# Durations from the trace as the prices of an emitter's clocks

## The chip, the cores and the metric

The kernel runs on one core of one Trainium2 chip. The metric is the device time of one execution in microseconds (us), and of several executions the median.

## The reference

One step of a hybrid trunk of two layers. It serves 1024 sample positions and 128 prompt positions, here side by side as 1152 columns of width D = 1024, all in float32. Layer 0 joins latent attention (MLA) and a two-way retention behind one input projection; layer 1 is a chunked gMLP. A SwiGLU channel mixer of width 2816 follows in each.

```python
for l in range(DEPTH):
    ... = ada_mod(c, w_ada[l], b_ada[l])
    hs = modulate(rmsnorm(xs, norm_g[l, 0]), sh1s, sc1s)
    if l % 2 == 0:
        ys = ab_latent(hs, cache_mla_ckv[:, j], ..., w_in_ab[j], w_uq[j], w_ukv[j], ..., w_o_ab[j])
    else:
        ys = chunk_gmlp(hs, w_in_c[j], ln_g_c[j], ..., w_out_c[j])
    xs = xs + g1s * ys
    hs = modulate(rmsnorm(xs, norm_g[l, 1]), sh2s, sc2s)
    xs = xs + g2s * swiglu(hs, w_ffn_gate[l], w_ffn_up[l], w_ffn_down[l])
y_sample = rmsnorm(xs, final_norm_g)
```

The prompt columns go through the same steps with their own modulation. In the attention of layer 0 the normed latents are multiplied by `w_uq` (queries) and `w_ukv` (keys and values).

## The kernel before

Each float32 operand of a product is kept as a high part and a low part, and each product of a tile is three matmuls (high by high, high by low, low by high). The high part is a ScalarE cast, the low part a VectorE (or GpSimd) subtraction. Weights come from memory through three staging buffers (`ST`) and are split into a ring of five (`w0` to `w4`). The columns are worked in chunks of 384 or in pieces of 288. The channel mixer uses a scheme of seven products on half-size blocks, whose operands are sums that VectorE and GpSimd prepare.

The program is emitted by Python functions, and each engine does its instructions in the order in which they were emitted. That order isn't written out by hand. `Clocks` (L45) keeps a clock for each engine (T TensorE, V VectorE, S ScalarE, G GpSimd, Y the transfers' issue, D the transfers): `Clocks.op` (L76 to L114) gives every emitted instruction a start (its operands ready, its output free, its engine free) and a price. `Timed` (L117) sits between the emitter and the engines, so nearly every instruction of the profile has its line, L129. Nothing else of the program's timing is decided by these clocks but the place of background work:

- `fill` (L361), called between products, adds steps of three queues of generators as long as the VectorE and ScalarE clocks are no more than `ahead` past TensorE's: 7.0 us as a rule, 3.0 in the first part of the mixer, 1.5 at its end. It asks `bg3` (sums of squares), then `bg2` (the query products `upq`, L1270), then `bg` (all else).

```python
now = max(clk.t["T"], clk.ready(aps))
if not q or max(clk.t["V"], clk.t["S"], clk.t["G"] - 1.0) > now + ahead[0]:
    continue
```

- `Stream.pump` (L234) splits a weight when its clock says that the transfer has landed.
- The first stage (`advance` and the loop behind it, from L1169) picks among its tasks the one that can start first.
- `drain` (L356) and `bg_step` (L349) do not ask the clocks: they emit what is left of a generator at once, where its result is needed.

`upkv` (L1228) makes the keys and values of the attention: 26 groups of three matmuls, each evicted from PSUM into one of three buffers (`KVB`) and stored from there to `knd`, `kncd`, `vd` or `vpd`. It is background work of `bg`; behind the four gate units of the retention stands `drain(ck["kvdone"])`. At the very end `last1` and `done1` (L2469, L2475) take sums of squares of the final columns, and multiply by the reciprocal root; `done1` of the first half of the columns is background work too, of the second half it is drained.

Of the kernel before, what the change touches and what calls it, by code (L numbers as in the profile page):

```python
# [7 lines left out]
F32 = mybir.dt.float32  # L8
# [34 lines left out]
class Clocks:  # L43
# [33 lines left out]
    def op(self, e, name, args, kw):  # L77
        aps = [a for a in list(args) + list(kw.values()) if hasattr(a, "tensor")]
        out = kw.get("out", aps[0])
        ins = [a for a in aps if a is not out]  # L80
        t = max(self.t[e], self.ready(ins, e), self.free([out], e))
        n = 1
        for d in (ins[0] if name == "reduce_max" else out).shape[1:]:
            n *= d
        if "dma" in name:
            self.t[e] = t + (0.4 if e == "S" else 0.06)
            size = n * out.shape[0] * 4
            t = max(t + DMA_LAT, self.t["D"])
            self.t["D"] = t + size / 360e3
            end, e = self.t["D"] + DMA_LAT, "D"  # L90
        else:
            if e == "T":
                c = n / 2400 * (2 if name == "transpose" else 4 if ins[0].dtype == F32 else 1) + 0.014
                if out.shape[0] == 32:
                    c /= 4
                if t < PE_COLD:
                    c *= 2
            elif e == "V":
                psum = any(a.space == bass.MemoryType.PSUM for a in aps)
                c = (0.13 if psum else 0.065) + n / 960 * (6 if name == "reciprocal" else 1)  # L100
            elif e == "S":
                c = max(0.09 + n / 1200, 0.19)
                f = next((a for a in args if a in TABLES), None) if name == "activation" else None
                if f and f != self.table:
                    self.table = f
                    t += 1.28
            else:
                c = 0.16 + n / 480
            self.t[e] = t + c
            end = t + c  # L110
        for k in self.keys(out):
            self.w[k] = end, e
        for a in ins:
            for k in self.keys(a):  # L114
                self.r[k] = max(self.r.get(k, (0.0, e)), (end, e))
# [17 lines left out]
def body(nc, tc, ap):  # L133
# [473 lines left out]
    def rplaces(c):  # L607
        if c == 0:
            free = [hq_place(z, 0) for z in range(8)] + [flat_place(HF[z // 2], z % 2) for z in range(6)]
            for op in range(7):  # L610
                RIGHT[op, c] = free[2 * op:2 * op + 2]
        else:
            for n, op in enumerate((0, 1, 3, 5)):
                RIGHT[op, c] = [hq_place(2 * n + g, 1) for g in range(2)]
# [18 lines left out]
    def rsplit(c, todo):  # L633

        b11, b21, b12, b22 = ([xp2(2 * q + g, c, h) for g in range(2)] for h in range(2) for q in range(2))
        src = (b11, b21, b22, b11, b12, b22, b21)
        diff = dict(T1=(b11, b12, b11), T3=(b12, b22, b12), T2=(b22, b22, b11), T4=(b21, b21, b22))
        for z in todo:
            for g in range(2):
                if z in diff:  # L640
                    V.tensor_tensor(*(a[g] for a in diff[z]), ALU.subtract)
                    yield
                    continue
                op = int(z[1])
                if z[0] == "C":
                    if c and g == 0 and op in (2, 4, 6):
                        RIGHT[op, c] = x_places(op // 2 - 1)
                    S.copy(R(RIGHT[op, c][g][:, 0]), src[op][g])
                else:
                    hi, lo = (RIGHT[op, c][g][:, a] for a in range(2))  # L650
                    V.tensor_tensor(R(lo), src[op][g], hi, ALU.subtract)
                    if g:
                        normed.add((op, c))
                    yield
# [1893 lines left out]
```

## Time and profile before

| | us |
|---|---|
| median of 3 runs | 2855.09 |
| lowest and highest run | 2851.97, 2859.27 |
| the profiled execution | 2860.08 |
| its span in the trace | 2858.0 |
| TensorE busy | 2702.6 |
| VectorE busy | 1789.8 |
| ScalarE busy | 1168.2 |
| GpSimd busy | 514.3 |

The profiled execution is one run of its own, above the slowest of the three others by 0.81 us. In the rows below PE is TensorE's matmul, PEld its weight load, DVE VectorE, ACT ScalarE, POOL GpSimd and SP the engine that issues most transfers. A time in square brackets is how long the engine was idle before the row, and behind the arrow stands what ended that. Tiles stand without the numbers of their buffers (`hq`, `h`, `x`, `SC`, `w`).

### The profile page before, as it was taken

What the parts mean: (1) busy time and instruction counts of PE and PEld (TensorE: products, weight loads), DVE (VectorE), ACT (ScalarE), POOL (GpSimd) and SP (SyncE); (2) the same over time, 40 slices, a digit from 0 to 9 for tenths busy, and PEclk for the clock granted to TensorE, in tenths of its full rate; (3) what the DMA queues carried; (4) which work ended last, traced back from release to release, by engine and by line L of the source; (5) the groups of instructions that cost most, each with busy time, mean ns of one, the idle gap of its engine ahead of it and who ended that gap; (6) DMA issues with size and microseconds to landing.
All of it is one profiled execution on the core that took longest, in us unless ns stands there. A gap on an engine that the chain in (4) does not pass through costs nothing.

```text
span 2858.0 us, 49003 instructions
## 1 busy us (share of the span) xinstructions
PE 2702.6 (95%) x18859; PEld 2552.9 (89%) x18859; DVE 1789.8 (63%) x3606; ACT 1168.2 (41%) x2389; POOL 514.3 (18%) x570
## 2 busy tenths in 40 slices
PE   7999998999999999999999999998999999999996
PEld 5987897988999999999899877798899999999995
DVE  5661234888577566655788772455666666558876
ACT  5542223777455333433322351234544343332224
POOL 1120012665200000000465400000000000016550
PEclk8999998999999999999999999999999999999997
DMA  9386425323523444447878442352344343578761
GB/s 299 85 267 206 138 72 167 88 75 90 159 90 116 160 152 160 159 151 252 279 222 270 139 162 81 96 169 90 111 125 161 111 160 122 187 259 270 230 208 67
DMA packets 455328, 457.67 MB, mean 160 GB/s; under 512 B 25963, under 2 KB 399478, under 8 KB 453558
## 3 DMA queue, kind: packets, MB, share of 16 engines
q1 hardware_dynamic: 400272, 360.83, 41.1%
q10 hardware_dynamic: 54822, 93.70, 8.9%
q8 instruction: 149, 2.44, 0.4%
q14 instruction: 85, 0.70, 0.1%
HBM read 312.52 MB, written 141.93 MB: 159 GB/s over the span
## 4 chain that ended last, share of the span: by engine, by line
PE 70%; DVE 10%; DMA 5%; ACT 4%; issue 3%; POOL 1%; ACTq 0%; SPq 0%; DVEq 0%; POOLq 0%
PE PS L129 70%; DVE x L129 4%; DVE SC L129 2%; DVE w L129 2%; DMA hcd<-SC 2%; ACT x L129 1%; ACT w L129 1%; ACT SC L129 1%; DVE hq L129 1%; DMA ST<-in_w_ada 1%; POOL ST L129 1%; DMA w<-krd 0%; DMA rgd<-SC 0%; DMA w<-knd 0%; DMA ST<-in_w_in_c 0%
## 5 line engine op out<-in xcount | busy, mean ns | idle before, releaser
L129 PE MATMUL PS<-hq,w 128*128 128x288 f32 (+1 forms) x10644 | 1554.4, 303 | 57.9 <-ACT w L129 15.9
L129 PEld LDWEIGHTS PS<-hq,w 128*128 128x128 f32 x10644 | 1492.1, 190 | 93.0 <-ACT w L129 21.2
L129 DVE TENSOR_TENSOR w<-ST,w 128x512 fp32r<-128x512 f32 (+3 forms) x539 | 384.2, 730 | 292.6 <-ACT w L129 288.0
L129 ACT CAST w<-ST 128x512 fp32r<-128x512 f32 (+3 forms) x717 | 375.3, 552 | 424.1 <-POOL ST L129 277.0
L129 DVE SCALAR_TENSOR_TENSOR x<-PS,mod,x 128x288 f32<-128x288 f32 (+2 forms) x944 | 389.2, 445 | 125.1 <-PE PS L129 120.2
L129 POOL TENSOR_TENSOR w<-ST,w 128x256 fp32r<-128x256 f32 (+1 forms) x178 | 126.3, 726 | 1591.8 <-ACT w L129 970.1
L129 PE MATMUL PS<-h,w 128*128 128x288 f32 (+1 forms) x2522 | 389.2, 299 | 9.6 <-DVE SC L129 6.3
L129 PEld LDWEIGHTS PS<-h,w 128*128 128x128 f32 (+1 forms) x2522 | 353.1, 190 | 20.2 <-DVE SC L129 8.8
L129 ACT COPY SC<-PS 128x576 f32<-128x576 f32 (+8 forms) x245 | 124.3, 510 | 266.6 <-PE PS L129 219.3
L129 PE MATMUL PS<-x,w 128*128 128x288 f32 (+1 forms) x1440 | 219.9, 300 | 3.0 <-ACT adac L129 2.0
L129 PEld LDWEIGHTS PS<-x,w 128*128 128x128 f32 x1440 | 204.4, 189 | 4.9 <-ACT h L129 2.4
L129 DVE TENSOR_TENSOR SC<-PS,SC 128x576 f32<-128x576 f32 (+3 forms) x145 | 93.6, 647 | 167.3 <-PE PS L129 152.0
L129 POOL TENSOR_TENSOR ST<-ST 128x256 f32<-128x256 f32 (+1 forms) x192 | 140.4, 731 | 151.5 <-DVE w L129 134.7
L129 PEld LDWEIGHTS PS<-w,hq 128*128 128x128 f32 x648 | 120.4, 188 | 38.8 <-issue 11.4
L129 PE MATMUL PS<-w,hq 128*128 128x512 f32 x648 | 154.5, 396 | 0.0
L129 DVE TENSOR_TENSOR SC<-SC 128x288 f32<-128x288 f32 (+5 forms) x215 | 104.9, 496 | 63.4 <-ACT SC L129 47.4
L129 ACT ACTIVATE SC<-SC 128x576 f32<-128x576 f32 (+2 forms) x89 | 56.9, 639 | 194.0 <-DVE SC L129 182.1
L129 PE MATMUL PS<-w,w 96*128 96x512 f32 x384 | 109.6, 421 | 6.2 <-DMA w<-krd 2.7
L129 DVE TENSOR_TENSOR SC<-SC,x 128x576 fp32r<-128x576 f32 (+1 forms) x90 | 68.1, 757 | 68.4 <-DMA hcd<-SC 50.0
L129 DVE TENSOR_REDUCE sm<-PS 128x1 f32<-128x1152 f32 (+1 forms) x72 | 89.1, 1237 | 25.7 <-PE PS L129 25.0
L129 ACT ACTIVATE SC<-x 128x288 f32<-128x288 f32 x128 | 55.2, 440 | 118.1 <-DVE x L129 95.6
L129 DVE TENSOR_TENSOR ST<-ST 128x512 f32<-128x512 f32 x144 | 98.9, 687 | 1.8
(191 smaller groups left out, 2486.1 us busy)
## 6 DMA issues: line engine op xcount, KB each, us to landing
hq<-hcd SPq DMA_DIRECT2D x106, 576.0 KB, 8.9
hcd<-x ACTq DMA_DIRECT2D x180, 288.0 KB, 2.2
ST<-in_w_ada SPq DMA_DIRECT2D x80, 512.0 KB, 4.2
h<-hcd SPq DMA_DIRECT2D x48, 576.0 KB, 7.2
ST<-in_w_ffn_gate SPq DMA_DIRECT2D x52, 512.0 KB, 3.9
ST<-in_w_ffn_up SPq DMA_DIRECT2D x52, 512.0 KB, 4.0
hcd<-SC ACTq DMA_DIRECT2D x72, 288.0 KB, 3.3
ST<-in_w_ffn_down SPq DMA_DIRECT2D x80, 256.0 KB, 5.0
```

The source lines that it names most:

```text
L129: return fn(*args, **kw)
```

## The change

Only the prices in `Clocks.op` change. A matmul costs at least 0.11 us; one whose output has 32 rows is priced as one pass and not as a quarter of its price. A VectorE instruction has 0.16 us plus a 960th of its elements, and 0.05 more with three inputs, in place of 0.13 (an operand in PSUM) or 0.065. A ScalarE instruction has 0.2 us plus elements by 1250, in place of 0.09 plus elements by 1200 and at least 0.19. GpSimd has 0.22 plus elements by 460, in place of 0.16 and 480.

```diff
             if e == "T":
-                c = n / 2400 * (2 if name == "transpose" else 4 if ins[0].dtype == F32 else 1) + 0.014
+                c = max(n / 2400 * (2 if name == "transpose" else 4 if ins[0].dtype == F32 else 1) + 0.014, 0.11)
                 if out.shape[0] == 32:
-                    c /= 4
+                    c = n / 2400 + 0.014
                 if t < PE_COLD:
                     c *= 2
             elif e == "V":
-                psum = any(a.space == bass.MemoryType.PSUM for a in aps)
-                c = (0.13 if psum else 0.065) + n / 960 * (6 if name == "reciprocal" else 1)
+                c = 0.16 + n / 960 * (6 if name == "reciprocal" else 1) + (0.05 if len(ins) > 2 else 0.0)
             elif e == "S":
-                c = max(0.09 + n / 1200, 0.19)
+                c = 0.2 + n / 1250
...
             else:
-                c = 0.16 + n / 480
+                c = 0.22 + n / 460
```

Each engine issues the same instructions as before, in another order in some stretches of the program. The file has one line fewer, so L129 becomes L128. Three places follow, before and then the change.

TensorE near the start: `S_92` is the modulation's condition vector (its products of 32 rows are the modulation quarters), `hq_13` and `hq_17` are parts of the normed input, `w_14` to `w_18` weights of the input projection. Before:

```order
L129 MATMUL PS<-hq_13_219,w_18_333 128x384 x6
L129 MATMUL PS<-hq_13_219,w_14_221 128x384 x6
L129 MATMUL PS<-hq_10_111,S_92 32x128 x32
L129 MATMUL PS<-SC,ones 128x384
L129 MATMUL PS<-ident,adac 128x128
L129 MATMUL PS<-hq_13_219,w_15_226 128x384 x6
L129 MATMUL PS<-hq_17_331,w_14_221 128x384 x6
L129 MATMUL PS<-hq_11_112,S_92 32x128 x32
```

and in the change:

```order
L128 MATMUL PS<-hq_13_219,w_18_345 128x384 x6
L128 MATMUL PS<-hq_10_111,S_92 32x128 x32
L128 MATMUL PS<-ident,adac 128x128
L128 MATMUL PS<-SC,ones 128x384
L128 MATMUL PS<-hq_11_112,S_92 32x128 x32
L128 MATMUL PS<-hq_13_219,w_14_221 128x384 x6
L128 MATMUL PS<-ident,adac 128x128
L128 MATMUL PS<-hq_13_219,w_15_226 128x384 x6
```

The last two quarters (`hq_10`, `hq_11`) now stand ahead of three input products that stood between and before them.

SP's queue where the key stores (`knd`) begin; `qud` and `qhd` are stores of the query products, `h_5`, `h_6`, `SC` the buffers stored. Before:

```order
L129 DMA knd<-h_6_72 256x1x384 x2
L129 DMA knd<-SC 256x1x384
L129 DMA knd<-h_6_72 256x1x384
L129 DMA qud<-SC 96x384
L129 DMA qhd<-h_5_71 192x1x384
L129 DMA qud<-SC 96x384
L129 DMA qhd<-h_5_71 192x1x384
L129 DMA knd<-h_6_72 256x1x384
```

and in the change:

```order
L128 DMA ST<-in_w_in_ab 128x2x512
L128 DMA h_7_73<-in_cache_mla_ckv 128x128
L128 DMA h_7_73<-in_cache_mla_krope 128x32
L128 DMA knd<-h_6_72 256x1x384 x2
L128 DMA knd<-SC 256x1x384
L128 DMA knd<-h_6_72 256x1x384 x2
L128 DMA knd<-SC 256x1x384
L128 DMA knd<-h_6_72 256x1x384 x2
L128 DMA vd<-SC 128x8x128
L128 DMA vd<-h_6_72 128x8x128 x2
L128 DMA vd<-SC 128x8x128
L128 DMA vd<-h_6_72 128x8x128 x2
```

The stores of keys and values stand in one run, and the query stores that stood between them are ahead of it or behind it.

VectorE at the end of the program: `x_156` to `x_159` hold the final columns, `SC` sums of squares and their factors; a multiply-add reads PSUM (the eviction), a `TENSOR_TENSOR` of `128x2x288` is a final multiply. Before:

```order
L129 TENSOR_TENSOR SC<-SC 128x288
L129 SCALAR_TENSOR_TENSOR x_158_22500<-PS,mod_94,x_158_22500 128x160
L129 SCALAR_TENSOR_TENSOR x_158_22500<-PS,mod_94,x_158_22500 128x128
L129 TENSOR_TENSOR x_157_22499<-x_157_22499,SC 128x2x288
L129 SCALAR_TENSOR_TENSOR x_159_22642<-PS,mod_94,x_159_22642 128x288 x2
L129 TENSOR_TENSOR SC<-SC 128x288 x13
```

and in the change:

```order
L128 SCALAR_TENSOR_TENSOR x_158_22500<-PS,mod_94,x_158_22500 128x128
L128 SCALAR_TENSOR_TENSOR x_159_22642<-PS,mod_94,x_159_22642 128x288 x2
L128 TENSOR_TENSOR x_156_22498<-x_156_22498,SC 128x2x288
L128 TENSOR_TENSOR x_157_22499<-x_157_22499,SC 128x2x288 x2
L128 TENSOR_TENSOR x_156_22498<-x_156_22498,SC 128x2x288 x2
L128 TENSOR_TENSOR x_157_22499<-x_157_22499,SC 128x2x288 x2
L128 TENSOR_TENSOR SC<-SC 128x288 x12
```

Seven final multiplies now stand between the last two evictions and the run of sums; before, one stood ahead of these evictions and the others further up.

## Rows read from the trace of the kernel before

**Rows 1.** The page, part 1: busy time, share of the span, instructions by engine.
```profile
PE 2702.6 (95%) x18859; PEld 2552.9 (89%) x18859; DVE 1789.8 (63%) x3606; ACT 1168.2 (41%) x2389; POOL 514.3 (18%) x570
```

**Rows 2.** Busy time by stretch: length, engines, granted clock, transfers' share, GB/s.
```profile
0.00:80.00 80.00, 57.07 (x473) 47.01 (x474) 43.80 (x104) 42.79 (x94) 13.08 (x18) 0.87 0.85 268
60.00:80.00 20.00, 16.15 (x77) 14.31 (x77) 16.12 (x29) 11.44 (x25) 8.98 (x9) 0.91 0.44 163
140.00:190.00 50.00, 46.70 (x251) 43.57 (x251) 35.58 (x63) 28.17 (x67) 18.28 (x15) 0.97 0.82 259
190.00:240.00 50.00, 41.57 (x228) 36.90 (x227) 16.93 (x30) 19.74 (x43) 3.68 (x5) 0.93 0.82 249
```

**Rows 3.** VectorE groups by form (busy, mean ns), and a row of its timeline.
```profile
L129 DVE SCALAR_TENSOR_TENSOR x<-PS,mod,x 128x288 f32<-128x288 f32 x528 | 267.4, 514 | 97.5 <-PE PS L129 93.4
...
2821.52 0.94 DVE L129 SCALAR_TENSOR_TENSOR x<-PS,mod,x 128x288 f32<-128x288 f32 x2
```

**Rows 4.** TensorE's timeline near 45 us; transfers issued from 33 us on.
```profile
44.45 2.62 PE L129 MATMUL PS<-hq,w 128*128 128x384 f32 x6 [2.40 <-ACT hq L129]
47.00 3.64 PE L129 MATMUL PS<-hq,S 128*32 128x128 f32 x64
...
DMA packets 2083, 2.65 MB, mean 353 GB/s; under 512 B 112, under 2 KB 1879, under 8 KB 2083
...
hq<-in_w_ada SPq DMA_DIRECT2D x4, 1024.0 KB, 13.1
...
L129 SPq DMA_DIRECT2D hq<-in_w_ada x4: 433/1651/2960, 33.7 to 37.9; - x4
```

**Rows 5.** ScalarE's timeline, 214 to 224 us: start, length, instruction, idle before.
```profile
214.43 0.37 ACT L129 CAST h<-PS 128x256 fp32r<-128x256 f32 x1 [0.48 <-ACT SC L129]
217.59 0.37 ACT L129 COPY SC<-PS 128x256 f32<-128x256 f32 x1 [2.79 <-DMA knd<-SC]
...
220.12 0.37 ACT L129 COPY h<-PS 128x256 f32<-128x256 f32 x1 [0.85 <-DMA knd<-h]
```

**Rows 6.** TensorE's weight loads at 221 us, among the last key and value groups.
```profile
220.93 0.29 PEld L129 LDWEIGHTS PS<-x 128*128 128x128 f32 x1 [5.80 <-ACT SC L129]
```

**Rows 7.** Transfers issued from 135 to 260 us: KB each, median us to landing.
```profile
vd<-h SPq DMA_DIRECT2D x6, 512.0 KB, 4.5
...
knd<-h SPq DMA_DIRECT2D x6, 384.0 KB, 5.7
...
knd<-h SPq DMA_DIRECT2D x2, 256.0 KB
kncd<-h SPq DMA_DIRECT2D x3, 128.0 KB, 6.6
```

**Rows 8.** TensorE's timeline, waits between 800 and 2070 us, one at a weight load.
```profile
816.66 3.73 PE L129 MATMUL PS<-hq,w 128*128 128x288 f32 x14 [4.08 <-DVE w L129]
...
882.30 2.12 PE L129 MATMUL PS<-hq,w 128*128 128x288 f32 x12 [2.85 <-ACT SC L129]
...
1645.06 1.06 PE L129 MATMUL PS<-hq,hq 128*128 128x288 f32 x6 [1.52 <-DVE x L129]
...
1670.56 1.73 PE L129 MATMUL PS<-hq,w 128*128 128x288 f32 x11 [0.79 <-DVE w L129]
...
2002.54 0.50 PEld L129 LDWEIGHTS PS<-hq,w 128*128 128x128 f32 x2 [9.70 <-ACT w L129]
...
2064.24 2.17 PE L129 MATMUL PS<-hq,w 128*128 128x288 f32 x9 [2.56 <-ACT SC L129]
```

**Rows 9.** VectorE's timeline at the end: final multiplies beside evictions.
```profile
2820.18 1.42 DVE L129 TENSOR_TENSOR x<-x,SC 128x576 f32<-128x576 f32 x2
2822.37 0.75 DVE L129 TENSOR_TENSOR x<-x,SC 128x576 f32<-128x576 f32 x1
```

**Rows 10.** ScalarE's timeline at the end: the first and the last of ten squares.
```profile
2834.83 0.43 ACT L129 ACTIVATE SC<-x 128x288 f32<-128x288 f32 x1
...
2842.93 0.43 ACT L129 ACTIVATE SC<-x 128x288 f32<-128x288 f32 x1
```

## The prediction

> **What bounds the kernel now.** First the page's table of engines [rows 1]: TensorE is busy 2702.6 of 2858.0 us, VectorE 63%, ScalarE 41%. The reader should see that all the idle time of TensorE together is 155 us, so a change that only moves instructions can win no more than the idle time of the stretches it touches, and can lose more. Second, the change's order beside the order before: every engine issues the same instructions, and they move in 0 to 240 us, 800 to 930, 1600 to 1750, 1985 to 2130 and behind 2800 us of the execution before. The attention, the retention and the steady part of both channel mixers keep their order; I cost them at nothing, since neither a wait nor a queue changes there. Third, the busy time by stretch [rows 2]: TensorE idles 22.9 us in the first 80 and 11.7 us between 140 and 240. Last, the timelines at the places where the order differs.
>
> **What the new prices do.** `fill` adds background work while the later of the VectorE and ScalarE clocks is at most 7 us past TensorE's. A multiply-add of 128x288 on VectorE is recorded with 514 ns, and two in a row take 0.94 us, so the second begins 0.43 us after the first [rows 3]. The old price of this shape with an operand in PSUM is 0.13 + 288/960 = 0.43, the spacing; the new one is 0.16 + 0.30 + 0.05 = 0.51, the record. So the new clock of VectorE runs ahead of the engine by some 0.08 us an instruction, the window closes earlier, and background work is placed later, up to the point where something forces it out at once (`drain`). The page "Perfetto Trace Analysis" of the Trainium skill (section "Optimizing Scalar/DVE Operations") speaks against this change in the same way: the latency a profile shows is about twice the engine's own overhead, since its second half overlaps the next instruction. By that rule the clocks before were the better ones and late placement costs; if instead the record were the occupancy, only the waits that go would count, which is the first rival. The trace agrees in direction (0.43 against 0.51), not in the factor.
>
> **Term 1, the start (0 to 80 us): +3.** In the change the four-column products of modulation quarters 2 and 3 stand ahead of three input products, and on VectorE the copy of a quarter's sums stands ahead of the scaled inputs for them. Before, TensorE waited 2.40 us for those inputs and then did the products before the quarters [rows 4]. The last of four loads for the two quarters was issued at 37.9 us and took 13.1 to land, until 51.0; two of 1 MB belong to the last quarter, so that quarter 2's had landed by about 45.1, at 353 GB/s [rows 4]. Its products took 3.64 us there at most, so TensorE is through with them by 48.7 and waits 2.3 us or more for the last load. The inputs behind it are VectorE work that now starts late. Bounds: 0, if the input products that follow catch up in the waits of 60 to 80 us; +6, if VectorE's chain (eight pieces of 0.34 to 0.55 us, some 3.5 us) stays exposed too. I take +3, the wait and a little of the chain, because VectorE is busy for 16.1 of the 20 us from 60 to 80 [rows 2] and has little room to catch up.
>
> **Term 2, the key and value products (140 to 240 us): +5.** `upkv` makes 26 groups of three products, each evicted by ScalarE and VectorE into one of three buffers and stored by a transfer; a buffer is free when its store has landed. Before, the groups are spread from 141 to 225 us between input products and query groups. With the new prices the query groups, which come first in `fill`, use up the window, and `drain(ck["kvdone"])` forces all 26 groups into one block. That the stores set the pace there can be read from the little of it that exists before: ScalarE waited 2.79 us and, two evictions later, 0.85 us for stores to land, and three evictions passed in 5.69 us, 1.9 us each [rows 5], and TensorE stood for 5.80 us [rows 6]. In the block TensorE fills seven PSUM banks and can go on with the next product when the 20th eviction is done, for which 17 stores must have landed: 8 of 384 KB, 6 of 512 KB and 3 that I take as 256, 128 and 256 KB [rows 7], 6.95 MB. At 259 GB/s, the rate of 140 to 190 us [rows 2], that is 26.8 us. The first eviction begins some 4.5 us after TensorE enters the block (an estimate): an activation, a weight's cast, three casts of normed inputs and a copy stand ahead of it on ScalarE. TensorE's own work in the block is 82 products, about 14 us. So it stands for 4.5 + 26.8 - 14 = 17 us in place of the 11.7 us that go: +5. Bounds: at 353 GB/s, the best stretch of transfers [rows 4], 10 us of standing, -2; at 1.9 us an eviction [rows 5], 28 us, +17. I take the rate, since the stores run back to back. SP is queued past too: the two small cache loads and four small stores stand between them, which the three buffers hide.
>
> **Term 3, the places with moved weights (800 to 2130 us): 0.** Waits of 4.08, 2.85 and 2.56 us on TensorE, four at the entry of layer 1 that make 5.4 together (the first 1.52, the last 0.79), and one of 9.70 us on its weight loads, go away [rows 8], because evictions and some casts now stand ahead of background work. What is late next, place by place: in the first output projection, the low parts of two later weights fall behind the row scaling, on a VectorE that is continuous there: +1.5. At the start of the mixer of layer 0 the prepared pieces of the second column block come 2.6 us too late: -1.5 in all. At the entry of layer 1, sixteen norm pieces of 0.43 us stand directly ahead of the products that read them, 4.8 us of new waits against 5.4 that go: -0.6. In the second output projection, another weight's low part is 5.6 us late and the statistics end at the same time as before: 0. At the mixer of layer 1, 2.6 go and 3.6 come: +0.6. Bounds: the waits that go without any new one, -24; and +8, if each of the two projections loses a further 4 us, as much as one late low part cost there before.
>
> **Term 4, the tail (behind 2800 us): +3.** Before, VectorE does the final multiplies of the first column block between evictions, 0.75 us recorded and 0.67 apart [rows 9], hidden beside products. In the change seven of the eight stand behind the last eviction of the last product, 7 x 0.67 = 4.7 us, and ahead of the sums of squares. ScalarE's squares alternate with those sums in two buffers, ten of them, one every 0.90 us, from 2834.83 to 2843.36 [rows 10], and everything to the end follows them. Two squares more are done early in the change, so the first sum begins after the multiplies, at about 2838.05, and the next square at 2838.5 in place of 2834.83: +3.65. Two small TensorE waits beside the moved multiplies go: -0.7. Bounds: +2, if the last eviction itself is 1.5 us earlier on a freer VectorE, and +4.
>
> **Sum.** 3 + 5 + 0 + 3 = +11 on the profiled execution's own 2860.08: 2871.1. The median of the three runs, 2855.09, lies 5.0 below it, so I forecast **2866 us**.
>
> **Rivals.** (a) The truer clocks only remove waits: no block of stores slows TensorE and nothing is late next. For it: the waits of rows 8 are real and their causes are moved out of the way. Against: the same rows of the order put other pieces late. Terms 1 and 2 at their lower ends (0 and -2), term 3 at -24, term 4 at +3: 2855 - 23 = 2832, faster. (b) Cancelling: the stores in the block reach 353 GB/s (-2), the start catches up (0), the tail alone costs 3: 2856, no change to be told. For it: TensorE's idle time in most of these places is small. It decides if the stores land within some 3.5 us each. (c) The block is slower than its bytes, at 1.9 us an eviction: +17 in place of +5, 2878; for it, the only piece of drain that the trace shows ran at that pace, though loads of 1.5 MB shared the transfers then.
>
> **Numbers.** A measurement of this kernel tells about 0.3%, 8.6 us, from no change: faster is below 2846.5, slower above 2863.7. Chances: forecast 0.44, (c) 0.10, (b) 0.30, (a) 0.16. The forecast's own range, 2858 to 2874, crosses 2863.7, with about 0.06 of its 0.44 below; slower is the other 0.38 and (c), 0.48, and same is (b) and the 0.06, 0.36. Faster is (a), 0.16. The range that leaves out a tenth at each end goes from 2844, inside (a), to 2883, above (c).
>
> **What would show it.** Right: 26 groups of the key and value products in one stretch from about 186 to 217 us, with ScalarE waiting for `knd` and `vd` stores and TensorE's busy share near a half; a wait of TensorE near 48 us on a load of `in_w_ada`; seven 128x576 multiplies in one run after the last eviction, and ScalarE's first square of the serial run some 3.6 us later against the last product. Waits of rows 8 gone, others of 2 to 6 us a few us on. Wrong: if TensorE's idle time between 140 and 240 stays at 12 us or falls, term 2 fails; if the stretches of rows 8 are shorter by more than 10 us together, term 3 does.

## The result, and the profile after

The changed kernel takes 2877.44 us (median of four runs, 2872.67 to 2882.33) against 2855.93 of the kernel before (four runs), a ratio of 1.0067 with a 95% interval of 1.0049 to 1.0085: slower by two thirds of a percent. The profiled execution took 2874.09 us, 14.0 above that of before.

The page of the kernel after has this for its span and its engines:

```profile
span 2872.2 us, 49010 instructions
...
PE 2706.7 (94%) x18859; PEld 2555.9 (89%) x18859; DVE 1790.0 (62%) x3606; ACT 1169.6 (41%) x2389; POOL 515.1 (18%) x570
```

Against [rows 1] all engines do the same work; the 14 us are TensorE's, as waits and as products at a lower clock. To find them I number the products in the order in which the program emits them (18078; the trace has 18859 records, as some plain float32 products stand in it twice) and subtract the start of the product with the same number. The difference grows and shrinks in these places (times of before):

| stretch | products | change of the difference, us |
|---|---|---|
| start and key groups, to 312 us | 0 to 1438 | +9.1 |
| attention, order nearly unmoved | to 4296 | -2.6 |
| output projection and first mixer units, 809 to 943 us | to 5172 | +7.4 |
| rest of the mixer, order nearly unmoved | to 10022 | +1.1 |
| entry of layer 1, 1610 to 1760 us | to 10744 | -4.8 |
| layer 1 to 2153 us | to 13214 | +1.2 |
| rest of its mixer, order nearly unmoved | to 17810 | +0.1 |
| tail | to the last product | +2.7 |

**The start.** TensorE's timeline after, against the waits of [rows 4]:

```profile
43.45 3.08 PE L128 MATMUL PS<-hq,S 128*32 128x128 f32 x60 [3.31 <-DMA hq<-in_w_ada]
...
49.54 1.94 PE L128 MATMUL PS<-hq,S 128*32 128x128 f32 x60 [0.69 <-DMA hq<-in_w_ada]
...
55.95 0.45 PE L128 MATMUL PS<-hq,w 128*128 128x384 f32 x1 [2.04 <-ACT hq L128]
```

TensorE stands for the modulation's loads as forecast, only for the load of quarter 2 rather than that of the last one, and then for the inputs behind them.

**The block.** The busy time by stretch, with the columns of [rows 2]:

```profile
140.00:190.00 50.00, 48.39 (x280) 45.90 (x280) 21.84 (x37) 19.62 (x42) 13.83 (x11) 1.00 0.62 192
190.00:240.00 50.00, 35.55 (x157) 29.75 (x157) 19.70 (x36) 20.63 (x48) 4.00 (x4) 0.80 0.78 241
```

and the first product of the block with three of TensorE's waits, then ScalarE's evictions beside them:

```profile
185.48 0.34 PE L128 MATMUL PS<-x 128*128 128x384 f32 x1
...
196.00 0.69 PE L128 MATMUL PS<-x 128*128 128x384 f32 x1 [3.90 <-DVE h L128]
...
205.33 0.50 PE L128 MATMUL PS<-x 128*128 128x512 f32 x1 [2.20 <-DVE h L128]
...
215.71 0.58 PE L128 MATMUL PS<-x 128*128 128x256 f32 x1 [3.98 <-ACT x L128]
```

```profile
199.00 0.48 ACT L128 CAST h<-PS 128x384 fp32r<-128x384 f32 x1 [2.68 <-DMA knd<-h]
200.01 0.48 ACT L128 CAST h<-PS 128x384 fp32r<-128x384 f32 x1 [0.53 <-DMA knd<-h]
201.03 0.48 ACT L128 CAST SC<-PS 128x384 fp32r<-128x384 f32 x1 [0.54 <-DMA knd<-SC]
204.21 0.48 ACT L128 CAST h<-PS 128x384 fp32r<-128x384 f32 x1 [2.70 <-DMA knd<-h]
```

TensorE idles 16.1 us between 140 and 240 in place of 11.7, nearly all of it among the 26 groups, where ScalarE waits for a store to land before most evictions. The transfers move 241 GB/s over these 50 us, and 277 from the block's first store until TensorE is nearly through:

```profile
196.00:221.00 25.00, 15.28 (x50) 11.26 (x51) 8.65 (x16) 8.07 (x18) 0.00 (x0) 0.64 0.87 277
```

And the granted clock falls from 0.93 to 0.80 of 2.4 GHz. That is a mix of its two levels, some 20 of the 50 us being at 1.2 GHz (50 x 0.20 x 2): at 196.00 the first product of a group takes 0.69 us, where the same form took 0.34 before the waits began (185.48).

**The mixer of layer 0.** TensorE has a wait of 5 us here that before does not have anywhere, and VectorE's rows tell why:

```profile
933.34 0.61 PE L128 MATMUL PS<-x,w 128*128 128x288 f32 x1 [5.21 <-ACT x L128]
```

```profile
930.12 0.46 DVE L128 TENSOR_TENSOR SC<-SC,adac 128x288 fp32r<-128x288 f32 x1 [1.59 <-ACT adac L128]
930.49 1.42 DVE L128 TENSOR_TENSOR hq<-x,hq 128x576 fp32r<-128x576 f32 x2
931.83 2.92 DVE L128 TENSOR_TENSOR x<-x,x 128x576 f32<-128x576 f32 x4
```

The last sums of the second column block (`x<-x,x`) are emitted only when the block's first product asks for them, behind VectorE's combining of the first block, which itself waits 1.59 us for a cast. Before, these sums were filling work, done at 884 to 889 us, some 250 products ahead of their use.

**The entry of layer 1.** Between 1645 and 1690 us one wait on TensorE is left of more than half a microsecond:

```profile
1669.92 0.40 PE L128 MATMUL PS<-hq,w 128*128 128x288 f32 x1 [1.79 <-ACT hq L128]
```

The four of before, 5.4 us, of which [rows 8] shows the first and the last, are gone.

**The tail.** VectorE, then ScalarE, behind the last eviction:

```profile
2843.48 0.52 DVE L128 SCALAR_TENSOR_TENSOR x<-PS,mod,x 128x288 f32<-128x288 f32 x1 [0.27 <-PE PS L128]
2843.91 4.76 DVE L128 TENSOR_TENSOR x<-x,SC 128x576 f32<-128x576 f32 x7
2848.59 1.42 DVE L128 TENSOR_TENSOR SC<-SC 128x288 f32<-128x288 f32 x3
```

```profile
2849.08 0.44 ACT L128 ACTIVATE SC<-x 128x288 f32<-128x288 f32 x1 [11.23 <-DVE SC L128]
...
2857.20 0.43 ACT L128 ACTIVATE SC<-x 128x288 f32<-128x288 f32 x1
```

The seven multiplies of [rows 9] take 4.76 us in one run, and the ten serial squares of [rows 10] begin 14.25 us after the first of these in before, of which 10.7 is the difference that had come about by then: 3.5 us more.

### The profile page after: what moved, and what is told of

Read it like the earlier page. It is cut to its first block, busy times and chain, and to the rows that moved or that the text cites. A ratio compares the mean times of both kernels' runs of the same rounds, so it can differ in the third digit from the quotient of the medians.

```text
span 2872.2 us, 49010 instructions
## 1 busy us (share of the span) xinstructions
PE 2706.7 (94%) x18859; PEld 2555.9 (89%) x18859; DVE 1790.0 (62%) x3606; ACT 1169.6 (41%) x2389; POOL 515.1 (18%) x570
## 4 chain that ended last, share of the span: by engine, by line
PE 62%; DVE 8%; DMA 4%; ACT 4%; issue 3%; POOL 1%; SPq 0%; ACTq 0%; DVEq 0%; POOLq 0%
PE PS L128 62%; DVE x L128 3%; DVE w L128 2%; DVE SC L128 2%; DMA hcd<-SC 1%; ACT x L128 1%; ACT w L128 1%; ACT SC L128 1%; DMA w<-krd 1%; POOL ST L128 1%; DMA x<-xtd 1%; DVE hq L128 1%; DVE ST L128 1%; DMA ST<-in_w_ffn_up 0%; DMA hcd<-x 0%
## 5 line engine op out<-in xcount | busy, mean ns | idle before, releaser
L128 PE MATMUL PS<-hq,w 128*128 128x288 f32 (+1 forms) x10644 | 1556.2, 303 | 45.1 <-ACT w L128 12.2
L128 PEld LDWEIGHTS PS<-hq,w 128*128 128x128 f32 x10644 | 1496.7, 190 | 79.4 <-issue 17.9
L128 ACT CAST w<-ST 128x512 fp32r<-128x512 f32 (+3 forms) x717 | 375.0, 552 | 438.6 <-POOL ST L128 287.8
L128 DVE TENSOR_TENSOR w<-ST,w 128x512 fp32r<-128x512 f32 (+3 forms) x539 | 380.8, 724 | 268.6 <-ACT w L128 264.1
L128 DVE SCALAR_TENSOR_TENSOR x<-PS,mod,x 128x288 f32<-128x288 f32 (+2 forms) x944 | 391.5, 445 | 137.8 <-PE PS L128 130.0
L128 POOL TENSOR_TENSOR w<-ST,w 128x256 fp32r<-128x256 f32 (+1 forms) x178 | 127.0, 730 | 1591.6 <-ACT w L128 963.2
L128 PE MATMUL PS<-h,w 128*128 128x288 f32 (+1 forms) x2522 | 386.1, 298 | 10.6 <-DVE x L128 5.4
L128 PEld LDWEIGHTS PS<-h,w 128*128 128x128 f32 (+1 forms) x2522 | 350.9, 189 | 20.8 <-DVE x L128 10.7
L128 ACT COPY SC<-PS 128x576 f32<-128x576 f32 (+7 forms) x249 | 126.2, 510 | 282.1 <-PE PS L128 231.5
L128 PE MATMUL PS<-x,w 128*128 128x288 f32 (+1 forms) x1440 | 220.5, 301 | 10.8 <-ACT x L128 7.7
L128 PEld LDWEIGHTS PS<-x,w 128*128 128x128 f32 x1440 | 204.6, 189 | 12.7 <-ACT x L128 8.4
L128 DVE TENSOR_TENSOR SC<-PS,SC 128x576 f32<-128x576 f32 (+3 forms) x145 | 93.6, 647 | 164.9 <-PE PS L128 159.7
L128 POOL TENSOR_TENSOR ST<-ST 128x256 f32<-128x256 f32 (+1 forms) x192 | 140.6, 732 | 156.1 <-DVE w L128 132.6
L128 PE MATMUL PS<-w,hq 128*128 128x512 f32 x648 | 156.6, 398 | 0.0
L128 PEld LDWEIGHTS PS<-w,hq 128*128 128x128 f32 x648 | 120.3, 188 | 40.1 <-issue 12.2
L128 DVE TENSOR_TENSOR SC<-SC 128x288 f32<-128x288 f32 (+5 forms) x215 | 105.4, 498 | 65.8 <-ACT SC L128 48.9
L128 ACT ACTIVATE SC<-SC 128x576 f32<-128x576 f32 (+2 forms) x89 | 56.9, 639 | 200.2 <-DVE SC L128 192.0
L128 PE MATMUL PS<-w,w 96*128 96x512 f32 x384 | 107.9, 416 | 5.1 <-DMA w<-krd 2.7
L128 DVE TENSOR_TENSOR SC<-SC,x 128x576 fp32r<-128x576 f32 (+1 forms) x90 | 68.0, 757 | 66.7 <-DMA hcd<-SC 47.4
L128 DVE TENSOR_REDUCE sm<-PS 128x1 f32<-128x1152 f32 (+1 forms) x72 | 89.1, 1237 | 24.0 <-PE PS L128 23.1
L128 ACT ACTIVATE SC<-x 128x288 f32<-128x288 f32 x128 | 55.2, 440 | 112.5 <-DVE x L128 87.1
L128 DVE TENSOR_TENSOR ST<-ST 128x512 f32<-128x512 f32 x144 | 98.9, 687 | 1.8
```

The lines of the kernel that those rows point to most:

```text
L128: return fn(*args, **kw)
```

## The experiments

Each edit stands on the file of the change or, the same, on that of before with both price lists and a count of the products emitted, so that the new prices can hold in one part of the program. In short form:

```diff
             if e == "T":
+                self.pe += 1
-            elif e == "V":
-                c = <new price>
+            elif e == "V":
+                c = <new price> if <condition> else <old price>
```

and so for the other engines. In the first four kernels the order outside the part named is that of before, and inside it that of the change (the third also moves some instructions between 2045 and 2112 us). Each kernel was timed in rounds with before on the same chip, where the median of before was 2862 to 2864 us; a difference in us is the ratio's.

**One stretch at a time.** Condition `self.pe < 1700`:

> The new prices hold for the first 1700 products only (up to the attention), the old ones behind. Theory (each stretch's cost is its own, and the sums of the stretches make the whole): the start and the one block of key and value groups cost what the change's trace shows there, +9.1 us at the entry of the attention less what is noise, so 7 to 10 us over the kernel before. Rival (the block is paid back before the attention by transfers that are then ahead, and the loss lies in the later stretches): within 3 us of before.

Measured: 2873.85 against 2863.91 us, ratio 1.0037 (1.0023 to 1.0051), +10.6 us. The theory holds.

Condition `3600 < self.pe < 9000`:

> The new prices between products 3600 and 9000 only: the output projection and the channel mixer of layer 0. Theory: +5 to +8 us, with a wait of about 5 us on the products of the mixer's second column block, whose prepared sums come on demand. Rival (my prediction's term: the two places cancel): -1 to +2 us.

Measured: ratio 1.0022 (1.0009 to 1.0035), +6.3 us, with the wait in its place on TensorE's timeline:

```profile
922.28 0.61 PE L136 MATMUL PS<-x,w 128*128 128x288 f32 x1 [5.09 <-ACT x L136]
```

The two places do not cancel. How much of it is the wait's and how much the output projection's was not timed apart; in the trace the output projection loses 1.9 us of the 8.1 that this part loses (products 4296 to 10022).

Condition `9000 < self.pe < 11100`:

> The new prices between products 9000 and 11100 only: the entry of layer 1 (its order moves a little in the second output projection too). Theory: 3 to 5 us faster than before, as the change's trace is there. Rival (the trace's gain is the spread of one execution, and my term of -0.6 holds): within 1.5 us.

Measured: 2854.70 against 2863.91 us, ratio 0.9962 (0.9948 to 0.9977), -10.9 us: a gain, and more than twice the -4.8 of the change's trace. The stretch of before is not the same in each execution. Its busy time by window (columns of [rows 2]) in before's own trace, in that of the next run, whose kernel has the order of before here, and in that of the whole change run again later:

```profile
1629.00:1680.00 51.00, 45.04 (x328) 42.60 (x329) 42.50 (x102) 25.92 (x50) 0.00 (x0) 1.00 0.34 110
```

```profile
1629.00:1680.00 51.00, 45.41 (x300) 43.85 (x301) 41.47 (x101) 23.40 (x47) 0.00 (x0) 0.90 0.32 106
```

```profile
1647.00:1695.00 48.00, 45.20 (x308) 43.12 (x312) 40.86 (x98) 22.12 (x45) 0.00 (x0) 0.93 0.34 112
```

From product 10100 to 10744 before's own execution takes 130.5 us, the next run's 135.2 with the same idle time of TensorE (9.0 us, before 8.9) at a lower clock, and the whole change's 127.0 with 5.4 us idle. The other traces agree: eight of the order of before take 130.4 to 130.5 us (four of them) or 133.6 to 135.2 (the other four), and five of the new order 126.2 to 127.0. So before was traced in a good execution here: 3.5 us are gained against that one, 8.2 against the worst, 5.8 between the means. The 10.9 timed (6.6 to 14.9) is more than this stretch gives in the traces; where the rest comes from is not shown.

Condition `self.pe > 16000`:

> The new prices from product 16000 on: the end of the second mixer and the final norm. Theory: seven final multiplies stand between the last eviction and the sums of squares and cost +2.5 to +4 us. Rival (the sums of squares can overlap them, or the freer VectorE ends the products earlier by as much): 0 to +1 us.

Measured: ratio 1.0010 (0.9999 to 1.0020), +2.9 us. The theory's size, though the interval takes in no change and the rival too. The traces decide: from product 17810 to the last, the three with the new order there take 2.6 to 3.2 us longer than before's, and nine others with the order of before between 0.8 us less and 2.0 more, in the mean 0.2 more.

**What in the start costs.** On the first of these kernels, the order in which `fill` asks its queues is turned:

```diff
-            for q in (bg3, bg2, bg):
+            for q in (bg3, bg, bg2) if clk.pe < 1700 else (bg3, bg2, bg):
```

> As the run with the new prices at the start only, but there `fill` asks the queue of the key and value products before that of the query products, so that their 26 groups stand spread over the input products again, as the order of this kernel shows. Theory (the one block, paced by its stores, is what the start costs): 0 to +3 us over the kernel before, the wait for the modulation's load being left. Rival (the block's cost is that of the whole shifted work, the query products' now as much as the keys' before): +7 to +11 us, as without this edit.

Measured: ratio 1.0008 (0.9998 to 1.0018), +2.3 us. In its trace the stretch to 240 us has waits elsewhere (one of 7.66 us at 176 us, as the input products there wait for ScalarE), but the clock is 0.97 between 190 and 240 us in place of 0.80 and the difference to before is 3.2 us at 254 us, past the block:

```profile
190.00:240.00 50.00, 45.05 (x247) 42.08 (x247) 21.68 (x40) 21.03 (x50) 9.95 (x10) 0.97 0.80 244
```

The interval of this run and that of the run without the edit lie apart: the block, not the new prices as such, makes most of the cost of the start.

The other way to spread the groups is a wider window:

```diff
-... > now + ahead[0]:
+... > now + (11.0 if clk.pe < 1700 else ahead[0]):
```

> As the run with the new prices at the start only, but `fill` may run 11 us ahead there in place of 7. Theory (the new prices do nothing but close the window earlier): the spread placement comes back with the wider window, and the time with it: 0 to +4 us over before. Rival (the order of single instructions, not the window, costs): +7 to +11 us.

Measured: ratio 1.0057 (1.0044 to 1.0071), +16.3 us. The theory falls here. The groups are spread again, but TensorE waits elsewhere, and ScalarE's row shows what for:

```profile
168.56 2.29 PE L136 MATMUL PS<-hq,w 128*128 128x384 f32 x6 [7.21 <-ACT SC L136]
```

```profile
165.10 1.57 ACT L136 CAST x<-h 128x384 fp32r<-128x384 f32 x3 [1.92 <-DVE h L136]
...
168.01 0.50 ACT L136 ACTIVATE SC<-PS 128x384 f32<-128x384 f32 x1
```

The eviction of the gate product (the ACTIVATE) stands behind the splitting of the latents, background work that waits for VectorE. The difference to before is 16.7 us by 242 us. A wide window lets through work that is not ready in time as well as the work that was missed.

Next, what sets the block's pace: its first eight groups get five buffers.

```diff
+        KNB = [HF[1][:, 0:768], HF[1][:, 768:1536], HF[1][:, 1536:2304], SC[:, 768:1536], SC[:, 1792:2560]]
-                    st = KVB[turn][:, 0:2 * n]
+                    st = KVB[turn % 3][:, 0:2 * n] if late else KNB[turn % 5]
```

The fifth buffer overlaps two of the query products' own, so part of the stored queries is changed by this kernel; the instructions are the same in number.

> As the run with the new prices at the start only, but the first eight key groups of the block are evicted into five buffers in place of three (the rest keep three). Theory of my prediction (the bytes of the stores set the pace at some 259 GB/s): ScalarE's waits for the `knd` stores come a few groups later and the block is as long: +8 to +12 us over before, as without this edit. Rival (it is each store's own 3.5 us to landing that is waited for, three at a time, and the transfers have room): the waits on the first eight groups, 8 us of TensorE's standing, fall by half or more: +3 to +7 us.

Measured: ratio 1.0024 (1.0011 to 1.0036), +6.9 us, between the two and too near to the 1.0037 without the edit to tell. The trace tells it. ScalarE's waits for stores come two groups later, and the first three of them are 1.2 to 1.9 us each:

```profile
198.44 0.86 ACT L136 CAST h<-PS 128x384 fp32r<-128x384 f32 x2 [0.96 <-DVE x L136]
199.18 0.88 ACT L136 CAST SC<-PS 128x384 fp32r<-128x384 f32 x2
201.98 0.48 ACT L136 CAST h<-PS 128x384 fp32r<-128x384 f32 x1 [1.91 <-DMA knd<-h]
203.70 0.48 ACT L136 CAST h<-PS 128x384 fp32r<-128x384 f32 x1 [1.24 <-DMA knd<-h]
205.86 0.48 ACT L136 CAST h<-PS 128x384 fp32r<-128x384 f32 x1 [1.68 <-DMA knd<-h]
```

From product 900 to 960 the kernel with three buffers takes 32.1 us, this one 31.5. With more stores in flight one takes longer to land: the fourth `knd` store took 5.8 us, in the kernel with three buffers 4.2. So two more buffers for the first eight groups hardly shorten the block. This bears out the prediction's idea: the rate of the stores holds it, and not the time of each. Why that rate is 244 GB/s in these 32 us (262 with five buffers), where 353 was seen before [rows 4], stays open.

**Which price.** The new prices of TensorE, ScalarE and GpSimd, VectorE's old:

> New prices for TensorE, ScalarE and GpSimd, VectorE at its old price, over the whole program. Theory (VectorE's price, the record in place of the spacing, costs the mixer and the tail and gives the gain at layer 1's entry, and at the start ScalarE's price alone makes the block too): +8 to +12 us, all of it in the first 240 us. Rival (VectorE's price makes the whole loss, as my prediction's text has it): within 3 us of before.

Measured: ratio 1.0050 (1.0036 to 1.0063), +14.3 us. The rival falls, and of the theory the part that all of the loss lies in the first 240 us. The start costs about as much with VectorE's old price (+8.8 us by 239 us in the trace), so the block needs no new price of VectorE. That ScalarE's, and not TensorE's or GpSimd's, makes it is argued, not run. Some 4.4 us more come in the first output projection; and at the entry of layer 1 the waits of [rows 8] stay, and the stretch takes 138.3 us:

```profile
1679.85 0.53 PE L136 MATMUL PS<-hq,w 128*128 128x288 f32 x2 [1.45 <-ACT w L136]
1681.17 7.69 PE L136 MATMUL PS<-hq,w 128*128 128x288 f32 x46 [0.78 <-DVE w L136]
```

So the gain at the entry needs VectorE's new price. The wait of 5 us in the mixer of layer 0 does too, since this kernel has none there, and so does the cost of the tail, which takes as long in this trace as in before's. What each price does alone was not timed.

**The whole again**, beside these:

> The whole change once more, beside the other runs on one chip. Theory (the stretches are independent, so that the four parts add up): +0.2 to +0.45% over before, the sum of the four parts run alone, with the second mixer's stretch not in it. Rival (the parts are worse together, or a stretch that no part had costs as much again): +0.55% or more, as at first.

Measured: ratio 1.0077 (1.0062 to 1.0092), +22 us. The parts run so far make +8.9, so the rival holds, and a further stretch had to be looked at.

**The mixer and layer 1.** In the run with the new prices between products 3600 and 9000, the window of the mixer's first part is widened by 1 us:

```diff
-            ahead[0] = 3.0
+            ahead[0] = 4.0 if clk.pe < 9000 else 3.0
```

> As the run with the new prices between products 3600 and 9000, but in the first part of the mixer `fill` may run 4 us ahead in place of 3, so that the last sums of the second column block stand ahead of the block's products again. Theory (these sums, left to be forced out on demand, are the loss; the new order ahead of them is a gain): the wait of 5 us on them is gone, and the whole is 1 to 5 us faster than before in place of 6 slower. Rival (the window's width is not what costs there, as at the start): +4 to +8 us.

Measured: ratio 1.0012 (0.9997 to 1.0027), +3.4 us: not the theory's gain, and too near to the +6.3 without the edit to tell from it. In the trace the wait of 5 us is gone, but the sums now stand ahead of combining work, and two other waits come some 30 us earlier:

```profile
889.32 1.86 PE L136 MATMUL PS<-hq,w 128*128 128x288 f32 x12 [0.83 <-DVE SC L136]
894.07 4.97 PE L136 MATMUL PS<-hq,w 128*128 128x288 f32 x24 [2.89 <-ACT SC L136]
```

From product 4296 to 10022 this trace loses 5.6 us on before, the one without the edit 8.1. The sums have a price in the new place too.

Conditions `4650 < self.pe < 4900 or 9000 < self.pe < 11100`:

> The new prices only between products 4650 and 4900 (the first column block of the mixer of layer 0) and 9000 and 11100 (the entry of layer 1), the old ones elsewhere. Theory (the parts add up): 10 to 16 us faster than before, 9 from the entry, the rest from the mixer. Rival (one execution's spread made the mixer's -4.7): 7 to 10 us faster.

Measured: 2852.74 against 2862.19 us, ratio 0.9962 (0.9950 to 0.9974), -10.9 us. The number lies in the theory's range, and its interval (7.4 to 14.3 faster) takes in the rival's; but the entry alone had been timed at the same 10.9, so nothing more shows for the mixer. In the trace it gains 4.7 us from product 4700 to 4800 and gives back 2.4 by product 5100; the 2.3 left are less than the interval can tell. This kernel and that with the new prices at the entry alone are faster than before and than the change.

Conditions `4650 < self.pe < 4900 or 9000 < self.pe < 15000`:

> As the run just above, with the new prices on to product 15000: the second output projection and the mixer of layer 1 too. Theory (the 13 us between the whole and the sum of its four parts lie in this stretch): 8 to 13 us slower than the run just above. Rival (my prediction's term, near 0 there, and the rest is a loss that the parts have only together): within 3 us of it.

Measured: ratio 0.9985 (0.9975 to 0.9995), so against the run above 1.0023, some +6.6 us: nearer to the theory. TensorE's weight loads in the second output projection show where the old wait of 9.7 us [rows 8] went:

```profile
1999.93 0.50 PEld L136 LDWEIGHTS PS<-hq,w 128*128 128x128 f32 x2 [5.09 <-ACT w L136]
...
2012.70 1.04 PEld L136 LDWEIGHTS PS<-ones,SC 128*96 128x96 f32 x6 [4.11 <-DVE SC L136]
```

and the next mixer has a new one like that of layer 0, of half its size:

```profile
2105.87 0.93 PE L136 MATMUL PS<-x,w 128*128 128x288 f32 x5 [2.36 <-DVE x L136]
```

The traces of these two runs part by 2.5 us from product 11400 to 13000, and by 3.1 more from 13214 to 17810, where their order is the same. The latter holds in the others too: with the new order ahead of it that stretch takes 632.3 to 635.3 us (three traces), with the old one, or nearly so, 628.3 to 632.2 (ten traces, before's own the longest). Why is not shown, and the interval of each run is 3 us to either side.

All parts, that of layer 1's mixer as the difference of two runs: +10.6 + 6.3 - 10.9 + 6.6 + 2.9 = +15.5 us, where the whole has +19 (first ratio) and +22 (second). Each part has an interval of 3 to 4 us to either side, so the two agree; whether the parts are a little worse together stays open.

## Why the prediction was right

The forecast was 2866 us, slower, in a range of 2844 to 2883; measured were 2877.44. The sum was +11 on the profiled execution, and the profiled execution rose by 14.0. The rest of the miss is the step from there to the median: I took off 5.0 us, because the profiled execution of before lay above its own runs. That of after lies 3.4 below its median. The step "the median of the three runs, 2855.09, lies 5.0 below it", carried over to the changed kernel, is the one that missed most. The wide range held; the forecast's own, 2858 to 2874, did not, and that 2877 is nearly the 2878 of rival (c) is chance, as that rival's pace did not come (below).

**What the new prices do.** That the record overstates the spacing held; that late placement costs held at the start, in the mixers and in the tail, but not at the entry of layer 1. And I named VectorE alone. ScalarE's casts show the same: 0.48 us recorded, two in 0.86, so the second begins 0.38 behind the first (the five-buffer run's rows above). The old price of that shape is 0.09 + 384/1200 = 0.41, the new one 0.51, and the run without VectorE's price made the same block. The passage cited from the Trainium skill ("Perfetto Trace Analysis", section "Optimizing Scalar/DVE Operations"), that a profiled latency is about twice the engine's own overhead because half of it overlaps the next instruction, is stated for both engines. The rows agree in direction on both (0.51 recorded against 0.43 apart, 0.48 against 0.38); the factor of two they do not show.

**Term 1, +3.** Right in kind: 3.31 us for the load of quarter 2 and 0.69 for the last, where I had TensorE through with quarter 2 by 48.7 and waiting 2.3 for the last. The difference to before is +1.7 at 92 us, in its bounds of 0 to +6.

**Term 2, +5.** The mechanism is the one forecast: one block, paced by stores, 16.1 us of standing between 140 and 240 where 17 had been worked out, against 11.7. That these two agree is partly luck, since the pieces were each too small and cancel: the first eviction begins 8.5 us after TensorE enters the block (185.5 to 194.0) in place of 4.5, the 20th is done 30.2 us later in place of 26.8, and TensorE's own 82 products take 22.8 us in place of 14. What was left out is the clock: its fall to 0.80 makes the block's own products longer, which brings the term to +7.4 in the trace. Both terms together were timed at +10.6, against +8.

**Term 3, 0.** The total is near (+6.3 - 10.9 + 6.6 = +2.0), and that is luck: the parts are not. "At the start of the mixer of layer 0 the prepared pieces of the second column block come 2.6 us too late: -1.5 in all" was mis-sized: they come 5.2 us too late, as the combining ahead of them waits for a cast, and the waits that go ahead of them are given back. "4.8 us of new waits against 5.4 that go" at the entry was wrong: one wait of 1.79 is left, TensorE is idle 5.3 us in that stretch in place of 8.9, and the entry gains 4.8 us in the trace and 10.9 timed, in place of 0.6. The opening rule, that moved instructions can win no more than idle time, leaves out the clock here: of the 8.2 us gained against the worst trace of the old order only 3.6 were idle time. The second output projection was right: 9.7 goes, 5.1 and 4.1 come. Together with the mixer of layer 1 it was timed at +6.6 all the same, in place of +0.6; in the traces 3.1 us of it lie behind the places where the order moves, and why is open.

**Term 4, +3.** Right: seven multiplies in 4.76 us (4.7), the first square 3.5 us later (3.65), +2.7 in the trace and +2.9 timed.

**The rivals.** (a) had a point at the entry alone, where waits go and nothing is late next. (b) needed the stores to land at 353 GB/s; the transfers moved 241 in 190 to 240 us and 277 in the block's busiest 25. (c), 1.9 us an eviction, did not come: three evictions take 5.2 us in the rows above, 1.7 each, for the 384 KB stores, and 37.4 us pass from the first of the 26 to the last (194.03 to 231.43), 1.5 each.

## What to carry to other kernels

A clock that places filling work needs the spacing at which an engine takes instructions, not the length that a trace records for one: two of a kind in a row, and the start of the second less the start of the first. Longer prices cost 0.7% here, though not everywhere: at the entry of layer 1 the order that they happened to make was the better one. Such a change is many changes in one; switch it on for one stretch of the program at a time, since here a gain of 11 us and losses of 26 stood under one ratio. And where filling work can be forced out at one point, read what that point would do with all of it at once.

## What was not expected of the hardware

- Waits can cost more than their length, through the clock that is granted behind them. In the block, 16 us of waits go with a granted clock of 0.80, and a 128x384 product takes 0.69 us in place of 0.34.
- The same order does not always get the same clock: the entry of layer 1 in the order of before was granted 1.00 in one execution and 0.90 in another, with the same idle time, and took 130.5 and 135.2 us. One trace of such a stretch can be 4.7 us too kind to a kernel, where the change moves it by 3.5 to 8.2.
- Five buffers in place of three for 384 KB stores moved the waits by two groups and shortened the block by 0.6 us of 32, while a store that had landed in 4.2 us took 5.8: at 244 to 262 GB/s the transfers were what was waited for.
